# Two row halves of a head pair alternate on TensorE, each half with a PSUM bank of its own

## The chip, the cores and the metric

The kernel runs on one core of one Trainium2 chip. The metric is the device time of one launch in microseconds, taken as the median of several runs. The profile is of one more execution of the same program.

## The reference, cut to what matters

A block of attention, state-space (SSD) and gated linear recurrence (LRU) mixers, then two decoder layers, each with a front (retention, RWKV-7 time mixing, a short convolution, gates, a merge) and a mixture of 32 experts. There are 256 tokens, the model is 1024 wide, and everything is float32. The change touches two places: the attention logits of the first block and the RWKV-7 recurrence of the two layers.

```
# fox_attention: 8 heads of 64, blocks of 128 queries
logits = einsum('bhqd,bhkd->bhqk', q_i, kt) * scale + (c_i[..., :, None] - ck[:, :, None, :])
logits = where(kpos <= qpos, logits, -inf)
p = softmax(logits); out = einsum('bhqk,bhkd->bhqd', p, vt)

# rwkv7_time_mix: 8 heads of 64, step by step over 256 tokens
sk = einsum('bhv k,bhk->bhv', state, kht)
state = state * wt - sk[..., None] * (at * kht)[:, :, None, :] + vt[..., None] * ktt[:, :, None, :]
y = einsum('bhvk,bhk->bhv', state, rt)
```

## The kernel before, in words

**Layout.** Channels of 512-wide activations lie as 4 tiles `j` of 128 partitions, so that each tile holds two heads of 64: head `2j` on partitions 0 to 63 (`u = 0`) and head `2j+1` on partitions 64 to 127 (`u = 1`). A matmul that contracts over one head's 64 channels uses 64 rows of TensorE's array; one whose output has 64 channels uses 64 columns. Others in the same places contract over 128 tokens and use all rows. A float32 matmul stands in the trace as two records.

**The RWKV recurrence** (`rwkv`) is done in two chunks `c` of 128 tokens. `KB` holds the scaled keys and removal keys, `PR` the scaled probes and receptances. Line 1541 builds the strict products N of one chunk (8 matmuls of 64 rows, 128 columns, 128 moved), four heads of one half per PSUM bank, and line 1542 masks each bank into memory on VectorE. `inverse` inverts a triangular matrix per head from 32-wide blocks (lines 1695 to 1746). Then, for each chunk, `scores` (line 1561, evicted by line 1562) is called three times: for `kp`, `kr` and `br`. Between them stand W1, the product X W1 (line 1589, evicted by line 1590 on ScalarE into SK), the state update and y.

- W1 is one bank in chunk 0 (line 1572). In chunk 1 each half has a bank: per head a 128-row product of `kp` and the values (line 1580), added to by a 64-row product of `PR` and the state S (line 1581), evicted per half by line 1582 on ScalarE.
- The state update (lines 1599 and 1600, chunk 0 only) has 128 rows, 64 columns, one bank, each head on its half of the bank's partitions.
- y (lines 1609, 1610 and, in chunk 1, 1612) is built in the same way in one bank: values with `kr` and SK with `br` (128 rows, 64 columns), then S with `PR` (64 rows, 64 columns).

**The logits** (`attention`, lines 1022 and 1023) are done for two query blocks `t` (128 keys in the first, 256 in the second) and two head groups `jj`. Per head a 128-row product adds the decay bias (line 1022), and a 64-row product of q and k is added to it (line 1023). Two heads of one half share a bank, and line 1024 adds the mask on VectorE while it evicts. Softmax, transposes and the product with the values (`po`, line 1045, evicted by line 1046 on VectorE) follow.

**Order of work.** Both chains are generators. `weave` takes one step of the chain, then one of the dense work (`proj`, `gates`, `dense`). A dense step is mostly `fm_pair` or `tm`: fp32r products (lines 560 and 562) of a weight that `unit` splits into two parts, on ScalarE (line 550) and VectorE (line 551). `ada` (line 1140) multiplies a chunk of modulation weights. `rank` sets a priority for some instructions, and the tile framework orders each engine's instructions by priority and by when it expects them to be ready; the order on the chip is the one in the trace.

**PSUM.** There are eight banks: four under the tag "mm" for the dense products, two under "acc", and two under "sm". `psb()` without a tag hands out the two "sm" banks in turn; all the changed code, `ada` and the small products of the chains use them. A bank is written again once its eviction is done.

**Loads.** Each 2 MB chunk of weights is loaded by SyncE's queue (line 435) into a place of memory that a planner chose beforehand from the order in which the program takes and frees memory; a load waits for the last use of its place. The changed code takes and frees no memory of that plan other than before.

Of the kernel before, what the change touches and what calls it, by code (L numbers as in the profile page):

```python
# [377 lines left out]
class Kernel:  # L378
# [6 lines left out]
    def C(self, name, i=0, n=None):  # L385
        for pack, at in self.cat.items():
            if name in at and pack in self.csts:
                o, w = at[name]
                return self.csts[pack][:, o + i:o + i + (w if n is None else n)]
        raise KeyError(name)  # L390
# [317 lines left out]
    def block1(self):  # L708
# [30 lines left out]
        u = self.unit(self.wfd.rearrange("p (k n) -> p k n", k=8), 8, 512)  # L739
# [42 lines left out]
        for m in (0, 2):  # L782
            p = self.fm_pair(w, act, m)
            for i in range(2):
                conv(p[:, i, :], e2("raw", 259, bufs=3), xc[:, m + i, :], m + i, "lcw", "lcb", 4)
        for c in range(3):
            w = self.get("w1", 1 + c)
            for m in (0, 2):
                p = self.fm_pair(w, act, m)
                for i in range(2):  # L790
                    j = 4 * c + m + i
# [211 lines left out]
        def attention():  # L1003
            qT, kT, vt = qkv[4], qkv[5], qkv[6]
            Ra = [big(4, 256) for i in range(2)]
            for i in range(2):
                V.tensor_tensor(Ra[i], RS[:, None, :].to_broadcast([128, 4, 256]),
                                C("ind", 4 * i, 4)[:, :, None].to_broadcast([128, 4, 256]), op=OP.mult)
            for t in range(2):
                n, S = t + 1, 128 * (t + 1)  # L1010
                for jj in range(2):

                    lg, PT = e2("lg", 4, 256)[:, :, 0:S], e2("PT", 4, 2, 128)
                    mx = self.small.tile([128, 4], F, name="mx")
                    sm = self.small.tile([128, 4], F, name="sm")
                    for u in range(2):

                        r = slice(64 * u, 64 * u + 64)
                        p = self.psb().rearrange("p (a s) -> p a s", a=2)
                        for i in range(2):  # L1020
                            j = 2 * jj + i
                            self.mm(p[:, i, 0:S], CS[:, t * 128:(t + 1) * 128], Ra[jj][:, 2 * i + u, 0:S], True, False)
                            self.mm(p[:, i, 0:S], qT[r, j, t * 128:(t + 1) * 128], kT[r, j, 0:S], False, True)
                        V.tensor_tensor(lg[:, u:u + 3:2, :], p[:, :, 0:S],
                                        C("negmask", 256 - S, S)[:, None, :].to_broadcast([128, 2, S]), op=OP.add)
                    V.tensor_reduce(mx, lg, axis=AX.X, op=OP.max, negate=True)
                    for h in range(4):
                        A.activation(lg[:, h, :], lg[:, h, :], AF.Exp, bias=mx[:, h:h + 1], accum_out=sm[:, h:h + 1])
                    V.reciprocal(sm, sm)
                    yield  # L1030
                    for h0 in range(0, 4, 4 // n):
                        p = self.psb()
                        pv = p.rearrange("p (h s q) -> p h s q", h=4 // n, s=n)
                        for i in range(4 // n):
                            for s in range(n):
                                T.transpose(pv[:, i, s, :], lg[:, h0 + i, s * 128:(s + 1) * 128], self.ident)
                        if h0:
                            V.tensor_copy(PT[:, h0:h0 + 4 // n, 0:n, :], pv)
                        else:
                            A.activation(PT[:, h0:h0 + 4 // n, 0:n, :], pv, AF.Copy)  # L1040
                    po = self.psb()
                    for i in range(4):
                        h = 4 * jj + i
                        for s in range(n):
                            self.mm(po[:, i * 64:(i + 1) * 64], PT[:, i, s, :], vt[:, s, h * 64:(h + 1) * 64], s == 0, s == n - 1)
                    V.tensor_tensor(by64(ya[:, t, jj * 256:(jj + 1) * 256]), by64(po[:, 0:256]), sm[:, :, None].to_broadcast([128, 4, 64]), op=OP.mult)
                    yield
            mem.done("lg", "PT")
            mem.free(*Ra, CS, RS, qT, kT, vt)
# [21 lines left out]
        for h in range(2):  # L1071
            p = self.psb().rearrange("p (j t) -> p j t", j=2)
# [359 lines left out]
    def rwkv(self, l, ys, lx, kx, rx, vx, lora):  # L1432
# [9 lines left out]
        for j in (0, 2):  # L1442
            for dst, src, lr, bias in ((sw, lx[0:64, 0, :], lora[0:64, 0:512], "w0"), (aa, lx[64:128, 0, :], lora[64:128, 0:512], "a0"),
                                       (gg, lx[:, 1, :], lora[:, 512:1024], None)):
                p = pair(self.psb())
# [14 lines left out]
        for j in (0, 2):  # L1460
            p = self.psb()
# [7 lines left out]
        for j in range(4):  # L1469
            for c in range(2):  # L1470
                s = slice(c * 128, c * 128 + 128)
# [18 lines left out]
        PR = big(4, 2, 2, 128)  # L1490
# [21 lines left out]
        vtok = big(2, 512)  # L1512
        for c in range(2):
            p = self.psb()
# [4 lines left out]
        for n, t in enumerate((ktok, btok)):  # L1519
            p = self.psb()  # L1520
# [13 lines left out]

        N = big(16, 128)
        for c in range(2):
            for u in range(2):
                r = slice(64 * u, 64 * u + 64)
                p = self.psb().rearrange("p (j t) -> p j t", j=4)
                for j in range(4):  # L1540
                    self.mm(p[:, j, :], KB[r, j, c, 1, :], PR[r, j, c, 0, :], True, True)
                V.tensor_tensor(N[:, 8 * c + u:8 * c + 8:2, :], p, C("strict")[:, None, :].to_broadcast([128, 4, 128]), op=OP.mult)
            yield
        Xs = []
# [9 lines left out]

        def scores(out, c, a, b, mask):

            for u in range(2):
                r = slice(64 * u, 64 * u + 64)
                p = self.psb().rearrange("p (j t) -> p j t", j=4)
                for j in range(4):  # L1560
                    self.mm(p[:, j, :], KB[r, j, c, a, :], PR[r, j, c, b, :], True, True)
                V.tensor_tensor(out[:, u::2, :], p, C(mask)[:, None, :].to_broadcast([128, 4, 128]), op=OP.mult)

        for c in range(2):
            kp = big(8, 128)
            scores(kp, c, 0, 0, "strict")
            yield
            W1, SK = big(512), big(512)
            if c == 0:
                p = self.psb()  # L1570
                for h in range(8):
                    self.mm(p[:, hs(h)], kp[:, h, :], vtok[:, c, hs(h)], True, True)
                A.activation(W1, p, AF.Copy)
            else:
                for u in range(2):
                    r = slice(64 * u, 64 * u + 64)
                    p = self.psb()
                    for j in range(4):
                        h = 2 * j + u
                        self.mm(p[:, hs(j)], kp[:, h, :], vtok[:, c, hs(h)], True, False)  # L1580
                        self.mm(p[:, hs(j)], PR[r, j, c, 0, :], S[r, j, :], False, True)
                    A.activation(W1.rearrange("p (j u v) -> p j u v", u=2, v=64)[:, :, u, :], p[:, 0:256].rearrange("p (j v) -> p j v", v=64), AF.Copy)
            mem.free(kp)
            kr, br = big(8, 128), big(8, 128)
            scores(kr, c, 0, 1, "incl")
            yield
            p = self.psb()
            for h in range(8):
                self.mm(p[:, hs(h)], X[:, 8 * c + h, :], W1[:, hs(h)], True, True)
            A.activation(SK, p, AF.Copy, scale=-1.0)  # L1590
            scores(br, c, 1, 1, "incl")
            yield
            if c == 0:
                p = self.psb()
                for j in range(4):
                    for u in range(2):
                        h = 2 * j + u
                        o = p[64 * u:64 * u + 64, hs(j)]
                        self.mm(o, ktok[:, hs(h)], vtok[:, 0, hs(h)], True, False)
                        self.mm(o, btok[:, hs(h)], SK[:, hs(h)], False, True)  # L1600
                V.tensor_tensor(S, p[:, 0:256].rearrange("p (j v) -> p j v", v=64), fin[:, :, None].to_broadcast([128, 4, 64]), op=OP.mult)
            y = ys["rwkv"] = ys["rwkv"] if c else big()
            p = self.psb()
            for j in range(4):
                for u in range(2):
                    h = 2 * j + u
                    r = slice(64 * u, 64 * u + 64)
                    o = p[r, j * 128:(j + 1) * 128]
                    self.mm(o, vtok[:, c, hs(h)], kr[:, h, :], True, False)
                    self.mm(o, SK[:, hs(h)], br[:, h, :], False, c == 0)  # L1610
                    if c:
                        self.mm(o, S[r, j, :], PR[r, j, c, 1, :], False, True)
            A.activation(y[:, :, c * 128:(c + 1) * 128], p.rearrange("p (j t) -> p j t", j=4), AF.Copy)
            mem.free(kr, br, W1, SK)
            if c == 0:
                mem.free(ktok, btok)
            yield
# [421 lines left out]
```

## Time and profile before

| | |
|---|---|
| median of 3 runs | 1937.93 us (1935.31 to 1941.15) |
| the profiled execution | 1933.05 us, span 1931.3 us |
| TensorE matmuls (PE) busy | 1619.3 us, 84% of the span |
| TensorE weight loads (PEld) | 1340.8 us, 69% |
| VectorE (DVE) busy | 949.7 us, 49% |
| ScalarE (ACT) busy | 559.5 us, 29% |
| GpSimd (POOL) busy | 26.7 us, 1% |
| read from HBM | 582.26 MB, 302 GB/s over the span |

The first block lasts about to 230 us, the front of the first layer to 640 us, its experts to 1105 us, the front of the second layer to 1465 us, and its experts to the end. Busy time is summed per engine, and an engine's records may overlap: two matmul records that run at once count once. The granted clock is given as a share of full speed, 2.4 GHz; its lower level is 0.5, 1.2 GHz.

### The profile page before, as it was taken

The numbers are of one execution on the slowest core, as the hardware profiler recorded it, in microseconds if no ns is written. First come the engines' busy times: TensorE is split into PE (matmuls) and PEld (weight loads), VectorE is DVE, ScalarE is ACT, GpSimd is POOL, SyncE is SP. The second block draws the span as 40 slices with busy tenths as digits, with TensorE's granted clock in tenths as the row PEclk, the third lists the DMA queues.
The fourth block names the chain that finished last, engine by engine and source line by source line (L and its number), as shares of the span: only waits on it lengthen the run. The fifth ranks groups of instructions, "written<-read, shape, count | busy, mean of one in ns | idle before, by whom it ended". The sixth has DMA issues, their size and how long they took to land. (4 is left out here: it accounts for less than half of the span.)

```text
span 1931.3 us, 42258 instructions
## 1 busy us (share of the span) xinstructions
PE 1619.3 (84%) x18830; PEld 1340.8 (69%) x18838; DVE 949.7 (49%) x2052; ACT 559.5 (29%) x858; POOL 26.7 (1%) x37
## 2 busy tenths in 40 slices
PE   6999999999999887775677799999998877756774
PEld 6778669878989775554555488889897655544553
DVE  7897656887438432221222368884384322212223
ACT  7736544623426200000000145344262000000001
POOL 0001000000000000000000000000000000000000
PEclk9999999999999898988888799999997998879898
DMA  8664654662337799999999956633377999999996
GB/s 334 233 225 160 236 215 166 257 253 98 132 110 291 287 426 424 426 426 425 427 427 426 425 196 260 255 124 132 104 290 284 425 426 425 427 426 426 426 425 260
DMA packets 43118, 586.11 MB, mean 303 GB/s; under 512 B 4816, under 2 KB 5456, under 8 KB 7984
## 3 DMA queue, kind: packets, MB, share of 16 engines
q1 hardware_dynamic: 41904, 579.72, 74.1%
q0 software_dynamic: 1024, 3.61, 0.5%
q8 instruction: 150, 2.46, 0.5%
q14 instruction: 40, 0.33, 0.0%
HBM read 582.26 MB, written 1.05 MB: 302 GB/s over the span
## 5 line engine op out<-in xcount | busy, mean ns | idle before, releaser
L560 PE MATMUL pst<-parts 128*128 128x256 f32 (+2 forms) x2896 | 444.3, 302 | 8.5 <-DVE parts L693 4.8
L560 PEld LDWEIGHTS pst<-parts 128*128 128x128 f32 (+1 forms) x2896 | 387.6, 193 | 46.1 <-issue 15.6
L1912 PE MATMUL pst<-memory,spare 128*32 128x128 f32 x6784 | 260.4, 318 | 145.1 <-DMA memory<-in_weu_dram 76.7
L1912 PEld LDWEIGHTS pst<-memory,spare 128*32 128x32 f32 x6784 | 230.7, 129 | 188.7 <-issue 119.1
L550 ACT ACTIVATE parts<-memory 128x1024 fp32r<-128x1024 f32 (+1 forms) x233 | 245.8, 1056 | 388.3 <-PE pst L560 322.2
L551 DVE TENSOR_TENSOR parts<-memory,parts 128x1024 fp32r<-128x1024 f32 (+1 forms) x233 | 283.7, 1220 | 146.5 <-ACT parts L550 138.9
L562 PE MATMUL pst<-parts 128*128 128x256 f32 (+2 forms) x1448 | 233.9, 298 | 3.3 <-DVE parts L551 3.3
L562 PEld LDWEIGHTS pst<-parts 128*128 128x128 f32 (+1 forms) x1448 | 199.2, 192 | 15.1 <-issue 4.8
L1932 DVE TENSOR_TENSOR spare<-pst,memory 32x256 f32<-32x256 f32 x256 | 107.6, 420 | 167.0 <-PE pst L1928 164.2
L1916 ACT ACTIVATE memory<-pst 128x128 f32<-128x128 f32 x64 | 25.1, 393 | 543.4 <-PE pst L1912 511.8
L1928 PE MATMUL pst<-memory 128*32 128x256 f32 x1696 | 118.4, 421 | 60.4 <-DMA memory<-in_wed_dram 41.5
L1928 PEld LDWEIGHTS pst<-memory 128*32 128x32 f32 x1696 | 61.0, 118 | 102.0 <-issue 57.2
L1865 PE MATMUL pst<-memory 128*128 128x128 f32 x512 | 126.0, 410 | 0.6 <-DVE memory L1859 0.6
L1865 PEld LDWEIGHTS pst<-memory 128*128 128x128 f32 x512 | 123.0, 334 | 4.4 <-issue 3.6
L1917 DVE TENSOR_TENSOR memory<-memory,pst 128x128 f32<-128x128 f32 x64 | 24.2, 378 | 204.6 <-ACT memory L1916 204.6
L1918 DVE TENSOR_TENSOR memory<-memory,pst 128x128 f32<-128x128 f32 x64 | 24.0, 375 | 189.7 <-PE pst L1912 189.5
L1868 ACT ACTIVATE spare<-pst,memory,gain 128x128 f32<-128x128 f32 x64 | 29.3, 458 | 191.0 <-DVE spare L1870 191.0
L1912 PE MATMUL pst<-spare 128*32 128x128 f32 x1408 | 49.8, 299 | 23.0 <-DMA spare<-in_weu_dram 11.3
L560 PE MATMUL po<-parts 128*128 128x512 f32 x256 | 65.4, 393 | 2.0 <-ACT parts L542 1.5
L1936 PE MATMUL acc<-spare,memory 128*128 128x512 f32 x128 | 59.7, 609 | 8.2 <-DVE spare L1932 8.2
L1912 PEld LDWEIGHTS pst<-spare 128*32 128x32 f32 x1408 | 44.2, 121 | 29.6 <-issue 22.4
L1870 DVE TENSOR_SCALAR spare<-pst,gain,memory 128x128 f32<-128x128 f32 x64 | 26.1, 408 | 64.8 <-PE pst L1865 55.5
(485 smaller groups left out, 1616.9 us busy)
## 6 DMA issues: line engine op xcount, KB each, us to landing
memory<-in_weg_dram SPq DMA_DIRECT2D x54, 2048.0 KB, 39.2
memory<-in_weu_dram SPq DMA_DIRECT2D x52, 2048.0 KB, 39.2
memory<-in_wed_dram SPq DMA_DIRECT2D x52, 2048.0 KB, 39.1
memory<-in_w_dram SPq DMA_DIRECT2D x33, 2048.0 KB, 8.7
memory<-in_ada_dram SPq DMA_DIRECT2D x24, 2048.0 KB, 8.2
memory<-in_wg_dram SPq DMA_DIRECT2D x12, 2048.0 KB, 8.0
spare<-in_weu_dram SPq DMA_DIRECT2D x12, 2048.0 KB, 39.2
spare<-in_wed_dram SPq DMA_DIRECT2D x10, 2048.0 KB, 40.2
```

Of the source, the lines that this page charges most:

```text
L550: self.nc.scalar.activation(hi, src, AF.Copy)
L551: self.nc.vector.tensor_tensor(lo, src, hi.bitcast(F), op=OP.subtract)
L560: self.mm(out, *((w[0], a[n]) if left else (a[n], w[0])), start and n == 0, False)
L562: self.mm(out, *((w[1], a[0]) if left else (a[0], w[1])), False, stop)
L1865: self.mm(p[:, i, :], self.x[:, t, j + i::8], S[:, t].rearrange("p e s -> p (e s)"), t == 0, t == 1)
L1868: A.activation(XG[:, j + i, :], p[:, i, :], AF.Identity, scale=gain(j + i), bias=shift(j + i))
L1870: V.tensor_scalar(XG[:, j + i, :], p[:, i, :], gain(j + i), shift(j + i), op0=OP.mult, op1=OP.add)
L1912: self.mm(ps[-1][32 * c:32 * c + 32, :], XG[:, j, s], w[:, j, 128 * c:128 * c + 128], j == 0, j == 7)
L1916: A.activation(hf, pg, AF.Sigmoid)
L1928: self.mm(p[32 * c:32 * c + 32, 0:256], h4[:, j, :], wd[:, j, 256 * c:256 * c + 256], j == 0, j == 3)
L1932: V.tensor_tensor(Y[r, s], p[32 * c:32 * c + 32, 0:256], gb[32 * c:32 * c + 32, s], op=OP.mult)
L1936: self.mm(acc[t][h], SWT[:, t * 128:(t + 1) * 128], Y[:, h * 512:(h + 1) * 512], False, e == 31)
```

## The change

Where a step has one bank per half, both banks are taken first, and the loop over `u` becomes the inner one, so that the matmuls of partitions 0 to 63 and 64 to 127 alternate; the evictions of both banks come after all matmuls of the pair. In the logits and W1 the 128-row matmuls of both halves come first, then the 64-row ones of both. In the state update and y, which keep their one bank, the order within a head pair becomes: the first product of both heads, the second of both, and in y the third of both. The matmuls, their operands and the evictions are the same in number and size.

```
-                    for u in range(2):
-                        r = slice(64 * u, 64 * u + 64)
-                        p = self.psb().rearrange("p (a s) -> p a s", a=2)
-                        for i in range(2):
-                            j = 2 * jj + i
+                    ps = [self.psb().rearrange("p (a s) -> p a s", a=2) for _ in range(2)]
+                    for i in range(2):
+                        j = 2 * jj + i
+                        for u, p in enumerate(ps):
                             self.mm(p[:, i, 0:S], CS[:, t * 128:(t + 1) * 128], Ra[jj][:, 2 * i + u, 0:S], True, False)
+                        for u, p in enumerate(ps):
+                            r = slice(64 * u, 64 * u + 64)
                             self.mm(p[:, i, 0:S], qT[r, j, t * 128:(t + 1) * 128], kT[r, j, 0:S], False, True)
+                    for u, p in enumerate(ps):
                         V.tensor_tensor(lg[:, u:u + 3:2, :], p[:, :, 0:S],
...
         def scores(out, c, a, b, mask):
-            for u in range(2):
-                r = slice(64 * u, 64 * u + 64)
-                p = self.psb().rearrange("p (j t) -> p j t", j=4)
-                for j in range(4):
+            ps = [self.psb().rearrange("p (j t) -> p j t", j=4) for _ in range(2)]
+            for j in range(4):
+                for u, p in enumerate(ps):
+                    r = slice(64 * u, 64 * u + 64)
                     self.mm(p[:, j, :], KB[r, j, c, a, :], PR[r, j, c, b, :], True, True)
+            for u, p in enumerate(ps):
                 V.tensor_tensor(out[:, u::2, :], p, C(mask)[:, None, :].to_broadcast([128, 4, 128]), op=OP.mult)
...
-                for u in range(2):
-                    r = slice(64 * u, 64 * u + 64)
-                    p = self.psb()
-                    for j in range(4):
-                        h = 2 * j + u
-                        self.mm(p[:, hs(j)], kp[:, h, :], vtok[:, c, hs(h)], True, False)
+                ps = [self.psb() for _ in range(2)]
+                for j in range(4):
+                    for u, p in enumerate(ps):
+                        self.mm(p[:, hs(j)], kp[:, 2 * j + u, :], vtok[:, c, hs(2 * j + u)], True, False)
+                    for u, p in enumerate(ps):
+                        r = slice(64 * u, 64 * u + 64)
                         self.mm(p[:, hs(j)], PR[r, j, c, 0, :], S[r, j, :], False, True)
+                for u, p in enumerate(ps):
                     A.activation(W1.rearrange("p (j u v) -> p j u v", u=2, v=64)[:, :, u, :], p[:, 0:256].rearrange("p (j v) -> p j v", v=64), AF.Copy)
...
-                    for u in range(2):
-                        h = 2 * j + u
-                        o = p[64 * u:64 * u + 64, hs(j)]
-                        self.mm(o, ktok[:, hs(h)], vtok[:, 0, hs(h)], True, False)
-                        self.mm(o, btok[:, hs(h)], SK[:, hs(h)], False, True)
+                    for n, (a, b) in enumerate(((ktok, vtok[:, 0]), (btok, SK))):
+                        for u in range(2):
+                            h = 2 * j + u
+                            self.mm(p[64 * u:64 * u + 64, hs(j)], a[:, hs(h)], b[:, hs(h)], n == 0, n == 1)
...
-                for u in range(2):
-                    h = 2 * j + u
-                    r = slice(64 * u, 64 * u + 64)
-                    o = p[r, j * 128:(j + 1) * 128]
-                    self.mm(o, vtok[:, c, hs(h)], kr[:, h, :], True, False)
-                    self.mm(o, SK[:, hs(h)], br[:, h, :], False, c == 0)
+                rs = [(slice(64 * u, 64 * u + 64), 2 * j + u) for u in range(2)]
+                o = [p[r, j * 128:(j + 1) * 128] for r, h in rs]
+                for u, (r, h) in enumerate(rs):
+                    self.mm(o[u], vtok[:, c, hs(h)], kr[:, h, :], True, False)
+                for u, (r, h) in enumerate(rs):
+                    self.mm(o[u], SK[:, hs(h)], br[:, h, :], False, c == 0)
+                for u, (r, h) in enumerate(rs):
                     if c:
-                        self.mm(o, S[r, j, :], PR[r, j, c, 1, :], False, True)
+                        self.mm(o[u], S[r, j, :], PR[r, j, c, 1, :], False, True)
```

N (line 1541) changes in the same way as `scores`.

## Rows read from the trace of the kernel before

**Rows 1.** Busy time in stretches: engines in us (records), granted clock, DMA share, GB/s.

```profile
540.00:560.00 20.00, 20.00 (x134) 18.61 (x134) 6.74 (x9) 3.67 (x6) 0.00 (x0) 0.83 0.25 86
590.00:600.00 10.00, 10.00 (x85) 10.00 (x84) 9.29 (x11) 9.08 (x12) 0.00 (x0) 1.00 0.26 67
760.00:1000.00 240.00, 165.24 (x2756) 128.59 (x2752) 57.58 (x160) 15.11 (x36) 0.00 (x0) 0.87 1.01 426
1360.00:1380.00 20.00, 20.00 (x131) 18.58 (x131) 6.42 (x8) 4.37 (x8) 0.00 (x0) 0.83 0.17 52
```

**Rows 2.** Waits of TensorE, 380 to 640 us: total us, times, longest.

```profile
PE pst L1702 <- issue: 3.4, 1, 3.4
```

**Rows 3.** Waits of SyncE's DMA queue, whole span: total us, times, longest.

```profile
SPq L435 <- DVE parts L551: 554.1, 48, 35.8
```

**Rows 4.** Timeline of TensorE, logits blocks of 128 and 256 keys: start us, us.

```profile
183.55 0.48 PE L1023 MATMUL pst<-memory 64*128 64x128 f32 x2
183.96 0.49 PE L1022 MATMUL pst<-memory 128*128 128x128 f32 x2
184.38 0.49 PE L1023 MATMUL pst<-memory 64*128 64x128 f32 x2
...
192.40 0.70 PE L1023 MATMUL pst<-memory 64*128 64x256 f32 x2
193.03 0.70 PE L1022 MATMUL pst<-memory 128*128 128x256 f32 x2
193.65 0.70 PE L1023 MATMUL pst<-memory 64*128 64x256 f32 x2
```

**Rows 5.** Timeline of VectorE at the same two blocks.

```profile
183.38 0.42 DVE L1046 TENSOR_TENSOR memory<-pst,sm 128x256 f32<-128x256 f32 x1 [0.29 <-PE pst L1045]
...
196.90 0.69 DVE L1024 TENSOR_TENSOR memory<-pst,memory 128x512 f32<-128x512 f32 x1 [1.82 <-PE pst L1023]
```

**Rows 6.** Timeline of TensorE at two of the twelve scores blocks.

```profile
501.97 1.71 PE L1561 MATMUL pst<-memory 64*128 64x128 f32 x16
503.61 1.82 PE L560 MATMUL pst<-parts 128*128 128x256 f32 x13
...
516.10 1.89 PE L1589 MATMUL pst<-memory 128*128 128x64 f32 x16
517.93 1.91 PE L1561 MATMUL pst<-memory 64*128 64x128 f32 x16
519.77 0.98 PE L560 MATMUL pst<-parts 128*128 128x256 f32 x6
```

**Rows 7.** Line 1590: duration min/median/max ns, first and last start us.

```profile
L1590 ACT ACTIVATE memory<-pst x4: 597/598/598, 518.0 to 1375.7; 128x512 f32<-128x512 f32 x4
```

**Rows 8.** Timeline of TensorE in W1 of chunk 1, and line 1582's durations.

```profile
540.50 0.43 PE L1580 MATMUL pst<-memory 128*128 128x64 f32 x2
540.86 0.43 PE L1581 MATMUL pst<-memory 64*128 64x64 f32 x2
541.22 0.43 PE L1580 MATMUL pst<-memory 128*128 128x64 f32 x2
...
L1582 ACT ACTIVATE memory<-pst x4: 384/384/384, 542.1 to 1366.4; 128x256 f32<-128x256 f32 x4
```

**Rows 9.** Timeline of TensorE: y of chunk 0, y of chunk 1.

```profile
526.69 0.44 PE L1609 MATMUL pst<-memory 128*64 128x128 f32 x4
...
528.59 0.38 PE L560 MATMUL pst<-parts 128*128 128x256 f32 x1
...
561.79 0.43 PE L1609 MATMUL pst<-memory 128*64 128x128 f32 x2
...
562.73 0.43 PE L1609 MATMUL pst<-memory 128*64 128x128 f32 x2
```

**Rows 10.** Timeline of TensorE: the first small product of the inverse.

```profile
458.43 1.29 PE L1695 MATMUL pst<-memory 32*32 32x32 f32 x128
```

**Rows 11.** The profile page's groups: busy us, mean ns, idle before.

```profile
L551 DVE TENSOR_TENSOR parts<-memory,parts 128x1024 fp32r<-128x1024 f32 (+1 forms) x233 | 283.7, 1220 | 146.5 <-ACT parts L550 138.9
```

More of the change, by code (lines that the diff above doesn't have):

```diff
@@ L1555, in scores @@
         def scores(out, c, a, b, mask):
-            for u in range(2):
-                r = slice(64 * u, 64 * u + 64)
-                p = self.psb().rearrange("p (j t) -> p j t", j=4)
-                for j in range(4):
+            ps = [self.psb().rearrange("p (j t) -> p j t", j=4) for _ in range(2)]
+            for j in range(4):
+                for u, p in enumerate(ps):
+                    r = slice(64 * u, 64 * u + 64)
                     self.mm(p[:, j, :], KB[r, j, c, a, :], PR[r, j, c, b, :], True, True)
+            for u, p in enumerate(ps):
                 V.tensor_tensor(out[:, u::2, :], p, C(mask)[:, None, :].to_broadcast([128, 4, 128]), op=OP.mult)
@@ L1574, in rwkv @@
             else:
-                for u in range(2):
-                    r = slice(64 * u, 64 * u + 64)
-                    p = self.psb()
-                    for j in range(4):
-                        h = 2 * j + u
-                        self.mm(p[:, hs(j)], kp[:, h, :], vtok[:, c, hs(h)], True, False)
+                ps = [self.psb() for _ in range(2)]
+                for j in range(4):
+                    for u, p in enumerate(ps):
+                        self.mm(p[:, hs(j)], kp[:, 2 * j + u, :], vtok[:, c, hs(2 * j + u)], True, False)
+                    for u, p in enumerate(ps):
+                        r = slice(64 * u, 64 * u + 64)
                         self.mm(p[:, hs(j)], PR[r, j, c, 0, :], S[r, j, :], False, True)
+                for u, p in enumerate(ps):
                     A.activation(W1.rearrange("p (j u v) -> p j u v", u=2, v=64)[:, :, u, :], p[:, 0:256].rearrange("p (j v) -> p j v", v=64), AF.Copy)
@@ L1604, in rwkv @@
             for j in range(4):
-                for u in range(2):
-                    h = 2 * j + u
-                    r = slice(64 * u, 64 * u + 64)
-                    o = p[r, j * 128:(j + 1) * 128]
-                    self.mm(o, vtok[:, c, hs(h)], kr[:, h, :], True, False)
-                    self.mm(o, SK[:, hs(h)], br[:, h, :], False, c == 0)
+                rs = [(slice(64 * u, 64 * u + 64), 2 * j + u) for u in range(2)]
[5 more added lines that the diff above has]
+                for u, (r, h) in enumerate(rs):
                     if c:
-                        self.mm(o, S[r, j, :], PR[r, j, c, 1, :], False, True)
+                        self.mm(o[u], S[r, j, :], PR[r, j, c, 1, :], False, True)
             A.activation(y[:, :, c * 128:(c + 1) * 128], p.rearrange("p (j t) -> p j t", j=4), AF.Copy)
```

## The prediction

> **What bounds the kernel now.** I read first the busy time of each engine in chosen stretches. In 540 to 560 us, where the changed code of the first layer stands, TensorE is busy for all 20.00 us while VectorE has 6.74 and ScalarE 3.67; 1360 to 1380 us, the same place of the second layer, looks alike [rows 1]. In 760 to 1000 us, the experts, the DMA engines are the bound (share 1.01, TensorE busy 165 of 240 us), and in 590 to 600 us, before the experts, the DMA has only 0.26 [rows 1]. So there are two regimes: fronts in which TensorE sets the pace, and expert stretches at the DMA's rate. Then the waits: the longest TensorE wait between 380 and 640 us is 3.4 us, "issue", in the small matmuls of the inverse [rows 2]; the changed lines are not in that list. Last the waits of SyncE's DMA queue: its largest total, 554.1 us, is for the second half of a weight split, L551 [rows 3]. A load waits until the front has used up a buffer, not the front for the load. I conclude that a microsecond taken from TensorE in a front moves all that follows, the expert loads too, by a microsecond.
>
> **Prices of TensorE.** A stream of fp32 matmuls (two records each) that fills the rows and 128 columns takes (517.93 - 516.10) / 16 = 0.114 us per record [rows 6]. The scores block that starts at 501.97 has two row halves of 8 records. One after the other they would cost 16 x 0.114 = 1.83 us beside the entry and exit; it takes 503.61 - 501.97 = 1.64 us [rows 6], so the halves already overlap at their seam. That two row halves can run at once is thus seen. Going from 128-row to 64-row matmuls and back costs: in the logits a pair of records takes 0.41 us and a pair of pairs 0.83 us [rows 4] where 4 x 0.114 = 0.46 would do, so 0.37 us for two changes, 0.19 each. In W1 a head takes 541.22 - 540.50 = 0.72 us [rows 8], 0.27 above 0.46, so 0.13 each.
>
> **N and scores (L1541, L1561).** Four N blocks (two chunks, two layers) and four first scores (kp) find both banks free. Interleaved, 8 slots of two records at 0.114 and one change of 0.19 give 1.10 us against 1.64: 0.54 x 8 = **4.3 us** saved. Six scores blocks (kr of chunk 0, br of both chunks, two layers) follow a single-bank product. There the second half waits for that bank: the block at 517.93 takes 519.77 - 517.93 = 1.84 us [rows 6], and the ScalarE copy that frees the bank starts at 518.0 and takes 0.598 [rows 7], so it is free near 518.65; 518.65 + 1.10 = 519.75. The second half sets the end already, and it starts no earlier after the change: **0**. Bounds: 0 if the wait stays, up to 1.84 - 1.10 = 0.74 each (4.4 us in all) if dense work is put into the wait; I take 0, because in the trace the block follows its product at once.
>
> **Logits (L1022, L1023).** Eight (bias, q) pairs at 128 keys, eight at 256. Now 0.83 us per pair at 128. After, per two heads: bias 0.41 + two more records 0.23, then the q pair at once 0.41, sum 1.05 against 1.66: 0.61 x 4 = 2.4 us. At 256 keys each pair of records takes 0.62 us [rows 4]; 0.62 + 2 x 0.23 + 0.62 = 1.70 against 2.49: 0.79 x 4 = 3.2. Gross 5.6. Against it stand two waits. Three of the four blocks follow a po product whose bank the second bias now needs after two records, not after half the block: L1046 starts at 183.38, takes 0.42 [rows 5], so the bank is free about 0.3 us later than wanted; 3 x 0.25 = 0.75. Two of the blocks are followed by an ada product that takes the next of the two "sm" banks. Now the first half's bank was emptied during the second half; after, TensorE must wait for an eviction of 0.42 or 0.69 us [rows 5] plus some 0.2 of hand-over: 1.5 us together. Net **3.4 us**, bounds 2 (a wait in each block) and 5.6 (none).
>
> **W1 of chunk 1 (L1580, L1581).** Per two heads: two kp matmuls, 4 x 0.114, then the PR pair at once, 2 x 0.114, two changes of 0.13: 0.95 us against 2 x 0.72 = 1.44. 0.49 x 8 = 4.0 us (4 head pairs, 2 layers). The kr scores behind it need both banks at once; the two L1582 copies of 0.384 us [rows 8], now one beside the second half's matmuls, come after both: one copy more on the path, 0.4 x 2 = 0.8. Net **3.2 us**, bounds 1.5 (both copies exposed) and 4.0.
>
> **State update and y of chunk 0 (L1599 to L1610): 0.** y of chunk 0 takes (528.59 - 526.69) / 32 = 0.059 us per record [rows 9], half of 0.114: the two column halves already overlap in the old order. The state update stands just ahead in the same form; bounds plus or minus 0.3 us.
>
> **y of chunk 1 (L1609 to L1612).** A head takes 562.73 - 561.79 = 0.94 us for six records [rows 9], as the two changes of form per head keep the halves apart. Paired, two heads go through the same chain at once: 0.94 per two heads, saved 0.94 x 8 = **7.5 us**. Bounds: 3.8 (half of the overlap) and 7.5. One rule speaks against a part of it. The two S matmuls lie in different row halves and write one bank. The row for this is L1695: 32-row matmuls in four row groups, all into one bank, 128 records in 1.29 us, 0.010 each [rows 10], which I read as overlap; I keep 7.5. The Trainium skill says in "TensorEngine Tiling (Array Packing)", Gotcha 1: PSUM Pressure, that different row tiles cannot access the same PSUM bank at the same time. By that rule the S pair would run one after the other and y would give 5.7 in place of 7.5; the trace speaks against it at 32 rows, and shows nothing at 64.
>
> **The granted clock.** In 540 to 560 and in 1360 to 1380 us it is 0.83 [rows 1]: 0.17 x 20 / 0.5 = 6.8 us at 1.2 GHz in each layer, right after W1 of chunk 1, whose 64-column matmuls leave the array mostly waiting for changes. At full clock that stretch would take about 3.8 us, as a record needs 0.114 against two times that at 1.2 GHz and some waits stay equal: 3.0 us per layer. After the change the thin stretch is some 4 to 5 us instead of 5.8, so the drop may stay or go: 0 to 6 us, and I take the middle, **3.0**.
>
> **Sum.** 4.3 + 3.4 + 3.2 + 7.5 + 3.0 = 21.4 us. Nothing is added on DMA or GpSimd, no instruction count changes, the evictions are the same ones, later. The profiled execution took 1933.05 us (span 1931.3), 4.9 below the median of the runs, 1937.93: for such an execution 1911.6, for the median **1916.5 us**.
>
> **Rivals.**
> *The second bank is not free in time and the old order comes back* (the change does not do what it says). The framework orders TensorE's instructions by priority and readiness, not by source alone; if it puts u = 0 first where a bank is late, only N, kp and y remain: 4.3 + 7.5 = 11.8, 1926. For it: the late banks above. Chance 0.14.
> *One bank cannot take two row halves*, so each S pair runs in turn: 2 records more, 0.22 us, for 8 pairs, 1.8 us: 1918.3. This is the rule named above; the 32-row matmuls speak against it. Chance 0.12.
> *Slower: each pair now holds both "sm" banks and TensorE stands before the next user.* 22 pairs (4 logits, 4 N, 12 scores, 2 W1). If each waits for a VectorE queue with one split, 1.22 us [rows 11], and an eviction of 0.69 [rows 5], that is 42 us against 5.6 + 4.3 + 4.0 + 7.5 = 21.4 gained without waits: 1958. It decides from 1.0 us of exposed wait per pair. Against it: dense L560 matmuls, which use the other banks, follow these blocks [rows 6]. Chance 0.06. The Trainium skill has the same concern ("TensorEngine Tiling (Array Packing)", PSUM Bottleneck): tiling speeds up TensorE and not the emptying of PSUM.
> *The gain ends in a DMA wait* before the experts, 1938. Against it: the share of 0.26 at 590 us and the queue's waits for L551 [rows 1, 3]. Chance 0.08.
> *More*: dense work fills the waits (4.4) and the clock stays up (3.0 more): 1909. Chance 0.06.
>
> **Numbers.** The forecast itself has 0.54. What can be told from no change is about 0.3%, 5.8 us. Faster: 0.54 + 0.14 + 0.12 + 0.06 = 0.86; same: 0.08; slower: 0.06. Range: from the forecast less 4.4, 3.0, the logits' 2.2 and 3 of scatter between runs, 1904, to the old-order rival and its scatter, 1930. Left out are the DMA and the slower case, 0.14, and what lies beyond the bounds.
>
> **What would show it.** Right: kp and N blocks of 16 records from 1.64 to about 1.1 us; kr and br unchanged near 1.84; y of chunk 1 from 7.5 to 3.8 us per layer; W1 from 5.8 to 3.8; expert loads as saturated as before and all earlier by 20 us. Wrong: runs of L1561 with eight records of one half first; waits of TensorE for L1024, L1562, L1582 of over a microsecond; S records of L1612 one after the other; a clock lower in other stretches; or a new gap before the first expert that eats the gain.

## The result, and the profile after

The changed kernel takes 1911.80 us (median of 4 runs, 1908.72 to 1915.78) where the kernel before takes 1937.89 (now 4 runs): 26.1 us less, a ratio of 0.9866 with a 95% interval of 0.9843 to 0.9888. A second measurement of the same two kernels, below, gives 0.9888 (0.9869 to 0.9907), 22.6 us less. The forecast was 21.4 us less, 1916.5, in a range of 1904 to 1930. The profiled execution took 1912.06 us (span 1910.3), 21.0 less than that of before.

First the same view as [rows 1], busy time in stretches of the changed kernel: engines in us (records), granted clock, DMA share, GB/s.

```profile
540.00:560.00 20.00, 20.00 (x187) 17.85 (x188) 7.55 (x9) 5.76 (x9) 0.00 (x0) 1.00 0.55 199
760.00:1000.00 240.00, 164.55 (x2744) 127.96 (x2740) 57.58 (x160) 15.12 (x36) 0.00 (x0) 0.86 1.01 426
1345.00:1365.00 20.00, 20.00 (x174) 19.02 (x173) 9.65 (x13) 5.81 (x9) 0.00 (x0) 1.00 0.19 59
```

TensorE is still busy all the time in the recurrence, but its clock is 1.00 where it was 0.83, in both layers. The experts are as they were.

Where the time went in the program is seen from the expert products, line 1912 before and 1917 after, asked for each layer's experts alone: duration min/median/max in ns, then the first and last start. First the kernel before, then the changed one.

```profile
L1912 PE MATMUL pst<-memory,spare x3392: 269/273/423, 662.2 to 1093.6; 128*32 128x128 f32 x200
L1912 PE MATMUL pst<-memory,spare x3392: 269/273/423, 1484.2 to 1912.5; 128*32 128x128 f32 x200
```

```profile
L1917 PE MATMUL pst<-memory,spare x3392: 269/273/423, 651.9 to 1083.6; 128*32 128x128 f32 x200
L1917 PE MATMUL pst<-memory,spare x3392: 269/273/423, 1464.3 to 1892.3; 128*32 128x128 f32 x200
```

The experts last 431.4 and 428.3 us before, 431.7 and 428.0 after. They start 10.3 us earlier in the first layer, and the stretch between the two (the second front) is 390.6 us before and 380.7 after, 9.9 less. So 20.2 of the 21.0 us by which the profiled executions differ were gained in front of the experts, and the loads handed them on.

Now the blocks, as they answer to [rows 4, 6, 8, 9]: the timeline of TensorE in the changed kernel, start us and us. Logits of 128 and of 256 keys:

```profile
173.13 0.68 PE L1021 MATMUL pst<-memory 128*128 128x128 f32 x4
173.75 0.49 PE L1024 MATMUL pst<-memory 64*128 64x128 f32 x4
174.17 0.71 PE L1021 MATMUL pst<-memory 128*128 128x128 f32 x4
...
175.23 0.50 PE L560 MATMUL pst<-parts 128*128 128x512 f32 x1
...
192.63 0.65 PE L1021 MATMUL pst<-memory 128*128 128x256 f32 x2
193.21 0.70 PE L1024 MATMUL pst<-memory 64*128 64x256 f32 x2
...
195.09 1.13 PE L1021 MATMUL pst<-memory 128*128 128x256 f32 x4
196.15 0.70 PE L1024 MATMUL pst<-memory 64*128 64x256 f32 x4
196.78 0.50 PE L560 MATMUL pst<-parts 128*128 128x512 f32 x1
```

The first block has the new order throughout: four records of a kind, then four of the other. The four 64-row ones take 174.17 - 173.75 = 0.42 us, as two did. The block lasts 175.23 - 173.13 = 2.10 us. The other begins in the old order, two and two, and ends in the new one. It takes 4.15 us, where it took 4.97 before and the forecast had 3.4 for the new order throughout.

A first scores block, then one that follows a single-bank product, then the end of W1 with the kr scores behind it:

```profile
501.41 1.16 PE L1564 MATMUL pst<-memory 64*128 64x128 f32 x16
502.50 0.39 PE L560 MATMUL pst<-parts 128*128 128x256 f32 x1
...
516.81 1.91 PE L1564 MATMUL pst<-memory 64*128 64x128 f32 x16
518.65 0.39 PE L560 MATMUL pst<-parts 128*128 128x256 f32 x1
...
540.20 0.66 PE L1582 MATMUL pst<-memory 128*128 128x64 f32 x4
540.79 0.44 PE L1585 MATMUL pst<-memory 64*128 64x64 f32 x4
541.16 0.62 PE L560 MATMUL pst<-parts 128*128 128x256 f32 x3
541.71 1.42 PE L1564 MATMUL pst<-memory 64*128 64x128 f32 x16
543.05 0.39 PE L560 MATMUL pst<-parts 128*128 128x256 f32 x1
```

The first kind of block falls from 1.64 to 1.09 us, and the second is unchanged at 1.84. W1 takes 541.16 - 540.20 = 0.96 us per two heads, where one head took 0.72. Three dense records now stand between W1 and the kr scores, which take 543.05 - 541.71 = 1.34 us.

y of chunk 1:

```profile
555.27 0.44 PE L1612 MATMUL pst<-memory 128*64 128x128 f32 x4
555.54 0.39 PE L1614 MATMUL pst<-memory 128*64 128x128 f32 x4
555.85 0.44 PE L1617 MATMUL pst<-memory 64*64 64x128 f32 x4
556.22 0.44 PE L1612 MATMUL pst<-memory 128*64 128x128 f32 x4
```

Two heads take 556.22 - 555.27 = 0.95 us, as one did [rows 9]. The four S records (line 1617), two row halves that write one bank, take 556.22 - 555.85 = 0.37 us. In the kernel before two S records took 562.73 - 562.37 = 0.36 us:

```profile
562.37 0.43 PE L1612 MATMUL pst<-memory 64*64 64x128 f32 x2
```

### The profile page after: what moved, and what is told of

Read it like the earlier page. It is cut to its first block, busy times and chain, and to the rows that moved or that the text cites. A ratio compares the mean times of both kernels' runs of the same rounds, so it can differ in the third digit from the quotient of the medians.

```text
span 1910.3 us, 42258 instructions
## 1 busy us (share of the span) xinstructions
PE 1596.2 (84%) x18830; PEld 1321.6 (69%) x18838; DVE 949.9 (50%) x2052; ACT 559.1 (29%) x858; POOL 26.5 (1%) x37
## 5 line engine op out<-in xcount | busy, mean ns | idle before, releaser
L560 PE MATMUL pst<-parts 128*128 128x256 f32 (+2 forms) x2896 | 444.9, 302 | 8.8 <-DVE parts L693 5.1
L560 PEld LDWEIGHTS pst<-parts 128*128 128x128 f32 (+1 forms) x2896 | 387.6, 193 | 47.0 <-issue 15.6
L1873 ACT ACTIVATE spare<-pst,memory,gain 128x128 f32<-128x128 f32 x64 | 29.3, 458 | 187.3 <-DVE spare L1875 187.3
L560 PE MATMUL po<-parts 128*128 128x512 f32 x256 | 66.1, 394 | 2.1 <-ACT parts L542 1.5
L1875 DVE TENSOR_SCALAR spare<-pst,gain,memory 128x128 f32<-128x128 f32 x64 | 26.1, 408 | 64.7 <-PE pst L1870 55.4
```

The lines of the kernel that those rows point to most:

```text
L560: self.mm(out, *((w[0], a[n]) if left else (a[n], w[0])), start and n == 0, False)
L1873: A.activation(XG[:, j + i, :], p[:, i, :], AF.Identity, scale=gain(j + i), bias=shift(j + i))
L1875: V.tensor_scalar(XG[:, j + i, :], p[:, i, :], gain(j + i), shift(j + i), op0=OP.mult, op1=OP.add)
```

## The experiments

**The two kernels again.** No edit. The question was whether the clock behind W1 falls by chance.

> The kernel before, once more, for a second trace. Theory A (the thin W1 block of chunk 1 brings TensorE's granted clock down right behind it): the clock is again at its lower level for some 7 us behind W1 of chunk 1 in both layers, windows of 540 to 560 and 1360 to 1380 us near 0.83 as before, and the kr scores behind W1 take about 2.8 us. Theory B (the drops there were chance): one or both of the two stretches show a full clock, and kr takes about 1.8 us. Block times elsewhere as before to 0.01 us: y of chunk 1 7.52 us, kp and N 1.64 us.

> The changed kernel once more, to narrow the size. Theory A (saved TensorE time of 18.4 us by block durations, and 6 us of clock): ratio near 0.987, 24 to 26 us less. Theory B (the block durations alone): 18 to 19 us less, ratio 0.990. The clock stays full behind W1 of chunk 1 in both layers by A; by B it may be down in one of them.

The kernel before took 1940.75 us in its one run, the changed one 1915.0 against 1937.62, ratio 0.9888 (0.9869 to 0.9907). In the second trace of the kernel before the clock is down behind W1 in both layers again:

```profile
543.00:563.00 20.00, 20.00 (x133) 18.64 (x133) 6.70 (x9) 4.07 (x7) 0.00 (x0) 0.83 0.22 74
1368.00:1388.00 20.00, 20.00 (x121) 18.29 (x121) 6.31 (x8) 3.12 (x7) 0.00 (x0) 0.74 0.15 46
```

The kr scores behind it take 2.8 us there, and all other blocks are as they were. In the second trace of the changed kernel the clock is full in both layers. So theory A holds for the old W1, with one correction: the drop can begin inside W1. In the three traces with the old W1 it lasts 6.8 to 10.2 us, and it begins between 2.9 us after the start of W1 and just behind its end. The size, 22.6 us, lies between the two that were set down (18 to 19 and 24 to 26), nearer to A; by itself it would not have decided.

**W1 alone in its old order.**

```
-                ps = [self.psb() for _ in range(2)]
-                for j in range(4):
-                    for u, p in enumerate(ps):
-                        self.mm(p[:, hs(j)], kp[:, 2 * j + u, :], vtok[:, c, hs(2 * j + u)], True, False)
-                    for u, p in enumerate(ps):
-                        r = slice(64 * u, 64 * u + 64)
+                for u in range(2):
+                    r = slice(64 * u, 64 * u + 64)
+                    p = self.psb()
+                    for j in range(4):
+                        h = 2 * j + u
+                        self.mm(p[:, hs(j)], kp[:, h, :], vtok[:, c, hs(h)], True, False)
                         self.mm(p[:, hs(j)], PR[r, j, c, 0, :], S[r, j, :], False, True)
-                for u, p in enumerate(ps):
                     A.activation(...)
```

> The changed kernel with W1 of chunk 1 alone in its old order. Theory A (the clock falls because of the old W1): W1 takes 5.6 to 5.8 us, the clock is at its lower level for some 7 us behind it in both layers, kr is longer than 1.35 us, and the time is 4.2 us (W1 and kr at full clock) plus up to 6 us (clock) above the changed kernel's: 8 to 10 us. Theory B (the clock fell by chance or from the whole order of the recurrence): W1 takes 5.8 us, the clock stays full in both layers, and the time is 4 to 5 us above.

The time is 1924.78 us, 9.8 above the changed kernel's 1915.0 on the same chip, and the ratio to the kernel before is 0.9929 (0.9912 to 0.9945), apart from the changed kernel's. The clock is down at W1 in both layers, and the scores behind it run at the pace of 1.2 GHz, 547.75 - 544.97 = 2.78 us for 15 records:

```profile
537.00:557.00 20.00, 20.00 (x121) 18.28 (x120) 6.32 (x8) 4.19 (x7) 0.00 (x0) 0.74 0.09 21
1357.00:1377.00 20.00, 20.00 (x131) 18.42 (x130) 6.32 (x8) 4.30 (x8) 0.00 (x0) 0.83 0.17 57
```

```profile
544.97 2.85 PE L1564 MATMUL pst<-memory 64*128 64x128 f32 x15
547.75 0.79 PE L560 MATMUL pst<-parts 128*128 128x256 f32 x2
```

This is theory A: the order of this one block is worth about 10 us, less than half of it by its own length and the rest by the clock.

**W1 alone in its new order**, on the kernel before (the same edit the other way).

> The kernel before with W1 of chunk 1 alone in the new order. Theory A (the thin old W1 brings the clock down; the new one does not): W1 takes 3.72 us, the clock stays full behind it in both layers, and the time is 8 to 10 us below that of before. Theory B (W1's own duration only): 4 to 5 us below, with the clock down behind W1 in at least one layer.

The time is 1931.52 against 1938.59 us, ratio 0.9962 (0.9948 to 0.9977). That is 7.1 us less, between the two theories. The trace says why: the clock is down behind the new W1 in the first layer and full in the second.

```profile
540.00:560.00 20.00, 20.00 (x144) 18.99 (x145) 7.39 (x9) 4.08 (x8) 0.00 (x0) 0.83 0.29 105
1362.00:1382.00 20.00, 20.00 (x164) 18.04 (x162) 8.20 (x10) 5.30 (x9) 0.00 (x0) 1.00 0.45 156
```

This run also gives the price of one drop, as its two layers execute the same 88 TensorE records from the start of W1 to the start of the br scores:

```profile
539.42 0.55 PE L1578 MATMUL pst<-memory 128*128 128x64 f32 x4
...
552.82 1.91 PE L1561 MATMUL pst<-memory 64*128 64x128 f32 x16
...
1361.09 0.55 PE L1578 MATMUL pst<-memory 128*128 128x64 f32 x4
...
1371.44 1.91 PE L1561 MATMUL pst<-memory 64*128 64x128 f32 x16
```

They take 13.40 us with a drop of 6.8 us and 10.35 without, so that drop costs 3.05 us.

So "the new one does not" was too strong. Over all traces of this study, the clock is down at the old W1 in 6 of 6 places (two traces of the kernel before and the run above), for 6.8 to 10.2 us. Behind the new W1 it is down in 6 of 14, five times for 3.4 us and once, here, for 6.8. With the denser W1 that has all its 128-row matmuls first (two runs, below) it is down in 0 of 4. What in the old W1 brings the clock down was not tested.

**y alone in its old order**, on the changed kernel.

> The changed kernel with y alone in its old order. Theory A (a front's TensorE time goes one to one into the end): y of chunk 1 is 7.52 us again in both layers, and the time is 7.4 us above the changed kernel's, 0.39%. Rival (the expert loads take part of the saving back): y is 7.52 us again, and the time rises by less than half of that, under 3.7 us.

The time is 1921.32 us, 6.3 above 1915.0, ratio 0.9911 (0.9894 to 0.9927), and y of chunk 1 takes 7.52 us again in both layers. That is 6.3 of the 7.4 us, and above the 3.7 that the rival allowed. The intervals of the two kernels overlap, and this trace has one drop of 3.4 us behind W1 that the two traces of the changed kernel do not have, so theory A is the likelier reading and not proven by this run.

**y grouped but not alternating.**

```
                 for u, (r, h) in enumerate(rs):
                     self.mm(o[u], vtok[:, c, hs(h)], kr[:, h, :], True, False)
-                for u, (r, h) in enumerate(rs):
                     self.mm(o[u], SK[:, hs(h)], br[:, h, :], False, c == 0)
```

> The changed kernel, but in y each head's values and SK products stand together again (first head both, second head both), and only the S products of the two heads stand side by side. Theory A (what cost time was the change between 128-row and 64-row matmuls behind each head; column halves overlap in any order): y of chunk 1 takes 3.8 to 3.9 us as in the changed kernel. Theory B (the strict alternation of the halves makes the overlap): the 128-row part of each pair takes twice as long, 0.44 us more per pair, so y takes about 5.6 us.

```profile
554.64 0.45 PE L1612 MATMUL pst<-memory 128*64 128x128 f32 x4
...
558.48 0.74 PE L560 MATMUL pst<-parts 128*128 128x256 f32 x4
```

y takes 558.48 - 554.64 = 3.84 us, where strict alternation has 3.81. So theory A holds: the column halves overlap in either order. What the old order lost was that each head's 64-row product stood between the 128-row products of the two heads. That a matmul adds to the result of the one before it is not what costs: in the old W1 the steps into the adding product and out of it to the next head are equally long, 0.36 us [rows 8].

**All 128-row matmuls of a block ahead of its 64-row ones**, in y, W1 and the logits. In each bank only the first matmul then opens the sum and only the last closes it. In W1, for example:

```
                 for j in range(4):
                     for u, p in enumerate(ps):
-                        self.mm(p[:, hs(j)], kp[:, 2 * j + u, :], vtok[:, c, hs(2 * j + u)], True, False)
+                        self.mm(p[:, hs(j)], kp[:, 2 * j + u, :], vtok[:, c, hs(2 * j + u)], j == 0, False)
+                for j in range(4):
                     for u, p in enumerate(ps):
                         r = slice(64 * u, 64 * u + 64)
-                        self.mm(p[:, hs(j)], PR[r, j, c, 0, :], S[r, j, :], False, True)
+                        self.mm(p[:, hs(j)], PR[r, j, c, 0, :], S[r, j, :], False, j == 3)
```

> The changed kernel, with all 128-row matmuls of a block before all its 64-row ones: in y of chunk 1, in W1 of chunk 1 and in the logits (one opening flag per bank in place of one per head). Theory A (each change between the forms costs 0.13 to 0.19 us): 6 of 8 changes fall away per W1 and per y, 2 of 4 per logits block. W1 from 3.72 to about 3.0 us, y from 3.81 to about 2.9 us, a logits block of 128 keys from 2.1 to about 1.7 us and of 256 keys to about 3.0 us: 1.5 + 1.8 + 3 to 4 us less than the changed kernel. Theory B (the overlap of halves is what counts, a change costs little once halves overlap): the blocks change by less than 0.3 us each and the time by less than 2 us.

The time is 1908.18 against 1938.59 us, ratio 0.9846 (0.9829 to 0.9863). This interval lies below that of the changed kernel's second measurement and overlaps that of the first. W1 and y of the first layer, timeline of TensorE:

```profile
532.92 1.89 PE L1583 MATMUL pst<-memory 128*128 128x64 f32 x16
534.75 1.11 PE L1587 MATMUL pst<-memory 64*128 64x64 f32 x16
535.78 0.62 PE L560 MATMUL pst<-parts 128*128 128x256 f32 x3
...
549.89 1.09 PE L1613 MATMUL pst<-memory 128*64 128x128 f32 x16
550.82 1.04 PE L1615 MATMUL pst<-memory 128*64 128x128 f32 x16
551.79 1.09 PE L1618 MATMUL pst<-memory 64*64 64x128 f32 x16
552.81 0.39 PE L560 MATMUL pst<-parts 128*128 128x256 f32 x1
```

W1 takes 2.86 us (3.0 expected) and y 2.92 (2.9); the four logits blocks take 1.70, 2.29, 2.94 and 3.76, together 2.4 us less than in the changed kernel, not 3 to 4. Theory A holds, with the price per change that the prediction had read: six changes fewer are 0.86 us in W1, 0.14 each, and 0.90 us in y, 0.15 each.

**A free bank for the pair.** First with three products moved to the dense tag, then with po left where it was. One of the edits, for X W1:

```
-            p = self.psb()
+            p = self.psb("mm")
             for h in range(8):
                 self.mm(p[:, hs(h)], X[:, 8 * c + h, :], W1[:, hs(h)], True, True)
```

> The changed kernel, with the products that stand right ahead of a pair (W1 of chunk 0, X W1, po) in a bank of the dense tag, so that both small banks are free when the pair starts. Theory A (the six kr and br blocks and three logits blocks gain nothing or little as the second half's bank is late): the six scores blocks go from 1.84 to 1.09 us, 4.5 us in all, the logits blocks of 2.68 and 4.16 us to 2.1 and 3.4 us, 2.2 us in all, and the time is 5 to 7 us below the changed kernel's. Theory B (dense work then waits for its fourth bank): the blocks get as short, but TensorE's waits for evictions at L560 grow, and the time is the same or longer.

> The changed kernel with only W1 of chunk 0 and X W1 in a bank of the dense tag; po stays in a small bank. Theory A (the run with po moved too lost its time in the attention alone, between 150 and 300 us): the attention is as in the changed kernel, the six scores blocks take 1.09 us as they did there, and the time is about 4.5 us below the changed kernel's. Theory B (dense work misses its fourth bank also in the fronts): TensorE waits or idles more between 490 and 580 us and eats the 4.5 us; the time is the same or longer.

With all three moved the kernel takes 1950.68 us, ratio 1.0068 (1.0044 to 1.0093): slower than the kernel before. The scores blocks did get short, 1.09 us in all six; the loss is elsewhere. The first kp block starts at 539.3 us, in the second trace of the changed kernel it starts at 500.6. Up to 150 us the two traces are alike (TensorE busy 95.52 and 95.57 of the 100 us before). The stretch behind shows where they part, with po moved and then in that second trace:

```profile
150.00:300.00 150.00, 122.44 (x611) 94.47 (x611) 74.52 (x144) 67.31 (x107) 8.96 (x12) 0.86 0.42 150
```

```profile
150.00:300.00 150.00, 146.64 (x815) 107.45 (x815) 98.11 (x194) 81.55 (x133) 10.15 (x12) 1.00 0.57 206
```

With po moved, TensorE is idle for 27.6 of these 150 us, and its clock is 0.86; in the changed kernel it is idle for 3.4. Its longest waits there (total us, times, longest) are for a norm (line 869) and the exponentials of the softmax (line 1030) and, as "issue", for nothing that the profile shows, with no dense work between:

```profile
PE pst L877 <- DVE memory L869: 6.1, 2, 5.8
PE pst L1021 <- issue: 5.7, 1, 5.7
PE pst L1038 <- ACT memory L1030: 4.3, 2, 3.4
```

Theory A fell by the time, and theory B by the place: the loss is not in TensorE's waits at L560 but in the order that the framework chose in the attention. Of the logits, the last block did come in the new order throughout, but the second and the third have other work between their matmuls. Why the framework chose that order is open. With po back in a small bank the attention is as in the changed kernel, and the six blocks keep their 1.09 us, as in the block whose first row stood at 516.81 above:

```profile
515.10 1.16 PE L1564 MATMUL pst<-memory 64*128 64x128 f32 x16
516.19 0.39 PE L560 MATMUL pst<-parts 128*128 128x256 f32 x1
```

The time is 1911.06 against 1940.37, ratio 0.9854 (0.9828 to 0.988). That is 29.3 us below the kernel before, where the changed kernel was 22.6 and 26.1 below. So the expected 4.5 us are seen in the lengths of the blocks. In the time the sign agrees, but the intervals overlap, and it decides nothing.

**Both edits together.**

> Both edits on the changed kernel: all 128-row matmuls of a block ahead of the 64-row ones, and W1 of chunk 0 and X W1 in a bank of the dense tag. If the two gains add (theory A): 1.6 us from the fronts' W1, 1.8 us from y, 2.4 us from the logits, 4.5 us from the scores, together 10 us below the changed kernel, ratio to the kernel before near 0.982. Theory B (either one shifts the order elsewhere or into waits): above 0.984.

The time is 1902.78 against 1940.37 us, ratio 0.9819 (0.9797 to 0.9841), the fastest of the study: 37.6 us below the kernel before, and its interval lies below both of the changed kernel's. The gains add, as theory A has it.

## Why the prediction was right

- **What bounds the kernel.** Right. What the fronts got shorter by, 10.3 and 9.9 us, went into the end, as the experts kept their length. So the rival of the DMA wait is out. The share of 0.26 at 590 us was thin evidence against it, as the DMA share is 0.97 at 600 to 620 us of the same trace.
- **The slower rival** did not come either. In the fronts of the changed kernel one wait is new, 0.5 us per layer, of ada for the mask on an N bank:

```profile
PE pst L1142 <- DVE memory L1545: 0.5, 1, 0.5
```

- **N and first scores.** The forecast was 4.3 us, by blocks that fall from 1.64 to 1.10. All eight fall from 1.64 to 1.09, 4.4 us.
- **Six scores blocks.** The 0 was right, and so was the reason, the bank: with the bank free they take 1.09. The record starts show more. In the changed kernel the second half begins 0.76 us into the block, after six records of the first, as before. The framework had kept the old order there, so the first rival came true in these six blocks.
- **Logits.** The size was right, 3.4 us net (3.30, 3.29, 4.97, 4.97 before; 2.10, 2.68, 4.15, 4.15 after), and the mechanism wrong. The step that failed is "against it stand two waits": no such wait is among TensorE's, and the ada product no longer follows at once. In its place three of the four blocks run partly in the old order. That this lost as much as the two waits would have is luck. The three follow a po product, so a late bank may be why; the run with po moved, which changed the whole attention, does not settle it.
- **State update and y of chunk 0.** The 0 was right: 0.98 and 1.90 us before, 0.98 and 1.85 after.
- **W1 and kr.** W1 takes 0.96 us per two heads against 0.95 in the forecast. The 0.8 us of exposed copies did not come: dense records fill that place.
- **y.** It falls from 7.52 to 3.81 us per layer, 7.4 in all against 7.5. By the rule of the Trainium skill that the prediction cites ("TensorEngine Tiling (Array Packing)", Gotcha 1: PSUM Pressure) the two row halves would not have written one bank at once. This case's trace does not agree: the four S records take 0.37 us, the time of two. That rival is out for halves that write different partitions of the bank, as here.
- **The clock.** This is the mis-sized term. 3.0 us was the middle of 0 and 6, and in both traces of the changed kernel both drops are gone. From the start of W1 to the start of the br scores, 88 records in every run, the two layers took 14.87 and 15.03 us before and take 10.05 and 10.05 after. That is 9.8 us for W1, kr and the clock together, where the forecast had 3.2 + 3.0 = 6.2. At 3.05 us for a drop of 6.8 about 6 of the 9.8 are the clock's. So the price of a drop, 3.0 us per layer in the forecast, was right, and the choice of the middle missed. The 3.6 us more are most of the 4.7 us by which the forecast fell short in the first measurement; with the second measurement (22.6) it fell short by 1.2. Behind the same W1 the drop still comes in 6 of the 10 places in other runs, so a middle was not unreasonable, and that the four places of the changed kernel have none may be luck. One premise was wrong: W1 does not leave the array "mostly waiting for changes", which by the prediction's own prices are 0.27 of 0.72 us per head.
- **The profile's own 21.0 us** is less than the medians' 26.1. The changed kernel's trace has a lower clock for 6.8 us near 104 us and for 3.4 us near 18 and near 1285 us, which the first trace of the kernel before does not have. The first two stand ahead of all changed code, and the second trace of the kernel before has 6.8 us near 104 and near 1299 us too, so they are not put down to the change.

## What to carry to other kernels

Look for a matmul that fills only some rows or columns, standing between two that could have overlapped: group by form first, and count the changes, here 0.13 to 0.19 us each. The two column halves of y did not have to alternate one by one to overlap (3.84 against 3.81 us). Two row halves with a bank each need both banks free at the start, or, as in six scores blocks here, the framework takes them in turn and nothing is gained (1.84 against 1.09 us). Try a bank freed for one block in the whole kernel: the order of everything near it is chosen anew, and one such edit lost more than the change had won.

## What the runs showed of the hardware that was not expected

The order of one short block can cost more through the clock than in the block: the old W1 lasts about 5.8 us at full clock and the new one 3.7, twice per execution, and yet the order is worth 9.8 us in the whole kernel. TensorE's granted clock goes to 1.2 GHz for 6.8 to 10.2 us in the old W1 or right behind it in 6 of 6 places, although the trace shows TensorE busy there all the time (20.00 of 20.00 us). Of two matmuls on different 64-row halves and the same PSUM bank, on different partitions, neither waited: 0.37 us for four records, where the two of one half alone take 0.36. What two row halves do that write the same partitions of one bank was not tried.
